# Differential heads of an encoder block: keys and values by seven products, one set of q and k

## The chip, the cores and the metric

The kernel runs on one core of a Trainium2 chip. The metric is device time in microseconds (us) of one execution, as the median of several runs. Shorthand for the engines is that of the profile: PE is TensorE (matmuls), PEld its weight loads, DVE is VectorE, ACT is ScalarE, POOL is GpSimd, SP is SyncE, which only issues DMAs here.

## The reference, cut to what matters

One residual layer on 512 tokens plus 16 meta tokens (528 rows), model width 1024, float32:

```python
xn = rmsnorm(h, norm_mix_g)
sb_q, sb_k, sb_v, df_q, df_k, df_v = split(xn @ w_in)        # six blocks of 1024 columns
# branch A: 8 stick-breaking heads of 128 columns: causal, no softmax
# branch B: 8 differential heads: two maps (c = 0, 1) of 64 columns each for q and k, one v of 128 columns
s = einsum(q, k) * 64 ** -0.5 - slope * |qpos - kpos|          # masked by chunks of 64 tokens
p = softmax(s)
w = p[:, :, 0] - lam * p[:, :, 1]
o = rmsnorm(w @ v, subln_g) * (1 - lam_init)
# both branches projected, gated, summed, w_out, residual; then SwiGLU (d_ff 2816), residual, final rmsnorm
```

## The kernel before, in words

Every float32 operand of a large product is split in two rounded parts (`split`, lines 75 to 79): ACT casts the number to `wh`, DVE subtracts to get `wl`. A product is then three matmuls (lines 272 to 274): high by high, high by low, low by high. `xT_h` and `xT_l` hold the normalised input, transposed: 8 blocks of 128 rows by 528 tokens.

The program runs through 8 stick-breaking heads, 8 differential heads (the loop `for br in range(2)` at line 984), the gates, the output projection, and the feed-forward part. While the scores, maps and outputs of head h are computed (`sb_head`, `df_head`), the projections of head h+1 are woven in as a list of units; at each `yield n` of the head generator n units are taken from the list. A differential head has:

- `scores(t)` for query blocks 0 to 2 and `scores3(c)` for block 3: matmuls of `q[c]` by `k[c]` into a PSUM tile `z`. The low parts lie in the other 64 partitions of `q[c]` and in a second row of `k[c]`, so two matmuls make a score.
- `biased`: one custom DVE instruction adds the bias and keeps the row maximum in `mx`.
- `maps(t)`: DVE negates the maximum (`nm`), ACT takes two exponentials with their sums, DVE makes the factors `rc`, scales map 0 and adds map 1.
- `attn_out`: transposes of the maps (`tr`), their split into `a_h` and `a_l`, and the product with v into another `z`.

The projections before: `halves(("df", h, 0))` makes q (24 matmuls of 512 columns), `kv_units` makes k and v, each in two halves of 264 tokens with 24 matmuls each. `q_evac` and `k_evac` write q and k from PSUM in 64-partition pieces (ACT the high part, DVE the low part), and when the last half of k is there, two DMAs on POOL's queue copy each `k[c]` into the other 64 partitions (`dk<-dk`, line 665). The scores of the head wait for those copies. Even heads keep q and k in `qh`, `ql`, `kh`, `kl` of the pool `att`; odd heads in one tile `dqk` in the place named `y_df`, so there are two sets.

From stick-breaking head 2 on (`SEVEN = 2`), k and v are made together by `seven_units`, a 2 by 2 block scheme with seven half-size products instead of eight (the blocks are the halves of the 1024 rows of the weights, the two matrices v and k, and the two halves of the tokens). Its weight operands are sums of weight blocks: `c1` splits the v chunk as it is, `c2` makes two sums on DVE and splits them, `c3` a third, `c4` a fourth (half a chunk). The token sums lie in `tA` and `tB`. A product is 12 matmuls of 264 columns. `seven_units` gives four units, u1 to u4; the DVE row `L219` is the second addition of `c2`, which reads the v chunk.

Weight chunks (512 KB) come in the order of the list `stream` by DMAs on SP's queue: `wst` has 3 places, `wsu` one place for the k chunk of a head with seven products. A place is free when the last split that reads it is done. The split parts have 4 places (`wh`, `wl`).

`y_units` are the branch projections of finished heads: ACT copies a PSUM tile to `y_out` (8 places, in the tile `y_sb`; `ys` and `sg` alternate before `y_out` exists), and POOL's queue adds it to a sum in DRAM. POOL's queue also issues `ds` transfers (line 137): sums of down-projection weights made by DMA in DRAM, one at every second unit until their list is empty, each held back until the split last written in the program has been cast.

The order on each engine is set by the framework's scheduler, which sorts by priority with its own estimate of durations. `tc.high_priority(offset=EVAC)` moves PSUM evacuations ahead. Each engine then works through its queue strictly in order, and so do the queues of SP and POOL.

## Time and profile before

| | us |
|---|---|
| median of 3 runs | 967.77 (967.52 to 967.91) |
| profiled execution, its own time | 967.45 |
| its span in the profile | 965.7 |
| PE busy | 948.0 (98%) |
| DVE busy | 705.2 (73%) |
| ACT busy | 588.9 (61%) |
| DMA engines, busy share per slice of 24 us, differential heads | 0.5 to 0.9 or more |
| from one `of` copy (line 740, once per differential head) to the next, six periods | 30.02 to 30.05 |

The page gives busy time per engine, the DMA queues, the chain of work that ended last, and the costliest groups of instructions. In a group the mean is that of one instruction; "idle before" is the time its engine stood still ahead of it. A PE row's duration includes the pipeline, so the distance of two starts, not the duration, is what a matmul costs in a row of matmuls. The differential heads run from about 261 to 500 us of the span.

### The profile page before, as it was taken

The page shows a single profiled execution, that of the slowest core. Times are in us where ns is not written, and L with a number is a line of the kernel's source. Part 1 is how long each engine was busy: PE and PEld are TensorE (multiplying, and loading weights), DVE is VectorE, ACT ScalarE, POOL GpSimd, SP SyncE. Part 2 cuts the span into 40 slices and gives each one's busy share as a digit, 9 for nine tenths or more (in the row PEclk, how much of TensorE's full clock was granted, in tenths as well). Part 3 has the DMA queues.
Part 4 walks back from the last instruction along what each step waited for, and adds up shares of the span by engine and source line. Part 5 has one row for each costly group of instructions (what it writes and reads, how often), then busy time and mean ns, then how long its engine had stood idle before and what let it go on. Part 6 is the DMA issues. An engine that isn't in the chain of part 4 may idle for free.

```text
span 965.7 us, 16166 instructions
## 1 busy us (share of the span) xinstructions
PE 948.0 (98%) x6118; PEld 853.7 (88%) x6118; DVE 705.2 (73%) x1292; ACT 588.9 (61%) x1130; POOL 185.2 (19%) x200
## 2 busy tenths in 40 slices
PE   8999999999999999999999999989999999999996
PEld 6988889898899889998888888879999999988885
DVE  7977777765577666877652553699888888999775
ACT  7765676666566666666774343585555555676564
POOL 3201111223234344322404540000000000000013
PEclk9999999999999999999999999999999999999999
DMA  8524655779989998856648853214434333276542
GB/s 243 153 71 127 184 169 177 158 164 213 189 182 188 190 205 188 187 116 123 130 112 207 272 181 104 68 46 144 115 88 123 96 108 111 67 254 204 183 156 88
DMA packets 151887, 146.88 MB, mean 152 GB/s; under 512 B 6113, under 2 KB 116866, under 8 KB 151810
## 3 DMA queue, kind: packets, MB, share of 16 engines
q1 hardware_dynamic: 132082, 98.46, 34.1%
q0 software_dynamic: 19568, 47.33, 24.3%
q8 instruction: 48, 0.79, 0.4%
q14 instruction: 29, 0.24, 0.1%
q10 hardware_dynamic: 160, 0.07, 0.0%
HBM read 122.11 MB, written 42.47 MB: 170 GB/s over the span
## 4 chain that ended last, share of the span: by engine, by line
PE 86%; DVE 8%; ACT 4%; issue 1%; DMA 0%; DVEq 0%; ACTq 0%; SPq 0%
PE mm L274 19%; PE mm L273 19%; PE mm L272 19%; PE z L272 7%; PE z L273 7%; PE z L274 7%; DVE wl L79 2%; PE z L683 1%; PE z L682 1%; PE z L538 1%; PE tr L538 1%; PE tr L514 1%; ACT wh L78 1%; DVE s L621 1%; PE z L566 1%
## 5 line engine op out<-in xcount | busy, mean ns | idle before, releaser
L272 PE MATMUL mm<-xT_h,wh 128*128 128x264 f32 (+2 forms) x656 | 214.6, 327 | 0.5 <-ACT xT_h L887 0.5
L273 PE MATMUL mm<-xT_l,wh 128*128 128x264 f32 (+2 forms) x656 | 213.3, 325 | 0.5
L274 PE MATMUL mm<-xT_h,wl 128*128 128x264 f32 (+2 forms) x656 | 212.6, 324 | 0.0
L79 DVE TENSOR_TENSOR wl<-wst,wh 128x1024 fp32r<-128x1024 f32 (+1 forms) x146 | 163.8, 1127 | 62.1 <-ACT wh L78 62.1
L78 ACT CAST wh<-wst 128x1024 fp32r<-128x1024 f32 (+1 forms) x146 | 140.0, 960 | 97.0 <-PE mm L273 64.9
L273 PEld LDWEIGHTS mm<-xT_l,wh 128*128 128x128 f32 x656 | 123.5, 188 | 10.2 <-DVE xT_l L888 1.3
L272 PEld LDWEIGHTS mm<-xT_h,wh 128*128 128x128 f32 x656 | 123.5, 188 | 9.9 <-ACT xT_h L887 0.9
L274 PEld LDWEIGHTS mm<-xT_h,wl 128*128 128x128 f32 x656 | 123.4, 188 | 9.9
L273 PE MATMUL mm<-hT_l,wh 128*128 128x256 f32 x284 | 80.5, 284 | 0.7 <-DVE hT_l L1133 0.7
L272 PE MATMUL mm<-hT_h,wh 128*128 128x256 f32 x284 | 80.3, 284 | 0.6 <-DVE sg L1228 0.6
L274 PE MATMUL mm<-hT_h,wl 128*128 128x256 f32 x284 | 80.1, 283 | 0.0
L1350 POOL TENSOR_TENSOR outs<-hres,gF 128x512 f32<-128x512 f32 x4 | 7.3, 1815 | 283.1 <-DVE hres L1336 278.0
L137 POOL DMA_DIRECT2D ds<-in_w_ffn_down_dram x36 | 28.5, 792 | 153.8 <-ACT wh L78 124.0
L686 DVE CUSTOM_DVE_ANT_0 pr<-z,bias 128x144 f32<-128x144 f32 (+3 forms) x64 | 30.9, 502 | 35.0 <-PE z L683 34.9
L273 PEld LDWEIGHTS mm<-hT_l,wh 128*128 128x128 f32 x284 | 53.7, 189 | 1.1 <-DVE hT_l L1133 1.1
L272 PEld LDWEIGHTS mm<-hT_h,wh 128*128 128x128 f32 x284 | 53.4, 189 | 0.9 <-DVE sg L1228 0.8
L274 PEld LDWEIGHTS mm<-hT_h,wl 128*128 128x128 f32 x284 | 53.5, 189 | 0.0
L272 PE MATMUL mm<-o_h,wh 128*128 128x512 f32 x128 | 53.1, 415 | 0.0
L272 PE MATMUL z<-wh,da 128*128 128x512 f32 (+1 forms) x132 | 50.9, 386 | 0.3 <-DVE hres L1336 0.3
L274 PE MATMUL mm<-o_h,wl 128*128 128x512 f32 x128 | 50.8, 397 | 0.0
L273 PE MATMUL mm<-o_l,wh 128*128 128x512 f32 x128 | 50.1, 392 | 0.3 <-DVE o_l L754 0.3
L273 PE MATMUL z<-wl,da 128*128 128x512 f32 (+1 forms) x132 | 50.2, 381 | 0.0
(346 smaller groups left out, 2562.7 us busy)
## 6 DMA issues: line engine op xcount, KB each, us to landing
wst<-in_w_in_dram SPq DMA_DIRECT2D x40, 512.0 KB, 5.9
ds<-in_w_ffn_down_dram POOLq DMA_DIRECT2D x30, 512.0 KB, 4.8
wst<-in_w_ffn_gate_dram SPq DMA_DIRECT2D x22, 512.0 KB, 4.0
wsu<-in_w_ffn_up_dram SPq DMA_DIRECT2D x21, 512.0 KB, 3.9
wst<-in_w_gate_dram SPq DMA_DIRECT2D x16, 512.0 KB, 4.5
y_df<-y_out POOLq DMA_DIRECT2D x32, 256.0 KB, 6.0
slots<-ds SPq DMA_DIRECT2D x13, 512.0 KB, 3.4
ds<-ds POOLq DMA_DIRECT2D x10, 512.0 KB, 7.4
```

The lines of the kernel that those rows point to most:

```text
L78: cast["last"] = (hi_copy or nc.scalar.copy)(hi, src)
L79: (lo_eng or nc.vector).tensor_tensor(lo, src, hi.bitcast(F32), op=ALU.subtract)
L137: tc.add_manual_dep(nc.gpsimd.dma_start(dst, src, **kw).ins, cast["last"].ins.name, paced)
L272: nc.tensor.matmul(ps, lhsT=ah, rhs=bh, start=(start and i == 0), stop=False, skip_group_check=skip)
L273: nc.tensor.matmul(ps, lhsT=ah, rhs=bl, start=False, stop=False, skip_group_check=skip)
L274: nc.tensor.matmul(ps, lhsT=al, rhs=bh, start=False, stop=(stop and i == n - 1), skip_group_check=skip)
L514: nc.tensor.transpose(pt[:, j * P:(j + 1) * P], vT[:, j * P:(j + 1) * P], ident)
L538: nc.tensor.transpose(pt[:, (t - j) * P:(t - j + 1) * P], blocks(t, j * P, (j + 1) * P), ident)
L566: nc.tensor.matmul(ps.rearrange("p (t q) -> p t q", q=P)[:, :, lo_rows:P], lhsT=vf[:, 1], rhs=a_s[:, 0:4 * qn], start=False, stop=True)
L621: nc.vector.tensor_tensor_scan(f, f, f, 0.0, op0=ALU.add, op1=ALU.bypass)
L682: nc.tensor.matmul(o, lhsT=q[c][:, qs], rhs=k[c][:, 0, k0:k1], start=True, stop=False)
L686: nc.vector.tensor_tensor_reduce(po, zz, bb, scale=1.0, scalar=-3.0e38, op0=ALU.add, op1=ALU.max, accum_out=mx[:, t, c:c + 1])
```

## The change

k and v of all eight differential heads are made by `seven_units`: chunks are streamed in the order v, k, q, with `c4` prepared right behind `c3`. q is projected after k and v instead of before. There is one set of q and k, in the pool `att`, for even and odd heads alike. `y_df` holds the token sums until the last head; `y_out` is made there only in the last iteration, so y tiles of the earlier ones go through `ys` and `sg`. Since `k_evac` in this scheme writes the second token half first, the copy DMAs are issued with the first half (`s.start == 0`). `seven_units` gives -k for that scheme's factor, hence the negated scores: `biased` scales by -1 and keeps a minimum, the exponentials use `scale=-1.0` and the minimum as bias, and the negation `nm` on DVE is gone. Map 0 is scaled on ACT instead of DVE.

```diff
-        for i in range(3):
+        for i in (2, 1, 0):
             cols(("df", h, i), w_in, (3 + i) * D + h * P)
...
     def sevens(key):
-        return key[0] == "sb" and key[1] >= SEVEN
+        return key[0] == "df" or key[0] == "sb" and key[1] >= SEVEN
...
-            fns = [c1, c2, c3] if key[2] else [generic, c4]
+            with_k = key[0] == "df"
+            fns = [c1, c2, c3] + [c4] * with_k if key[2] else [generic] + [c4] * (not with_k)
...
-        if h % 2:
-
-            both = opool.tile([P, 4 * L + 2 * SEQ], F32R, tag="y_df", name="dqk", bufs=1)
...
+        q = [ap_.tile([P, SEQ], F32R, tag=("qh", "ql")[c], name=f"dq{c}") for c in range(2)]
+        k = [ap_.tile([P, 2, L], F32R, tag=("kh", "kl")[c], name=f"dk{c}") for c in range(2)]
...
-                if s.stop == L:
+                if s.start == 0:
                     nc.gpsimd.dma_start(k[c][hs[1 - c]].bitcast(F32), k[c][a].bitcast(F32))
...
-        return d, halves(("df", h, 0), xT, QT, q_evac) + kv, turn
+        return d, kv + halves(("df", h, 0), xT, QT, q_evac), turn
...
-            nc.vector.tensor_tensor_reduce(po, zz, bb, scale=1.0, scalar=-3.0e38, op0=ALU.add, op1=ALU.max,
+            nc.vector.tensor_tensor_reduce(po, zz, bb, scale=-1.0, scalar=3.0e38, op0=ALU.add, op1=ALU.min,
...
-            nm = small.tile([P, 2], F32, tag="nm", name="nm")
-            nc.vector.tensor_scalar(nm, mx[:, t], -1.0, None, op0=ALU.mult)
             for c in range(2):
-                nc.scalar.activation(pr[:, c], pr[:, c], AF.Exp, bias=nm[:, c:c + 1], accum_out=ls[:, t, c:c + 1])
+                nc.scalar.activation(pr[:, c], pr[:, c], AF.Exp, scale=-1.0, bias=mx[:, t, c:c + 1], accum_out=ls[:, t, c:c + 1])
...
-                nc.vector.tensor_scalar(pr[:, 0], pr[:, 0], rc[:, 0:1], None, op0=ALU.mult)
+                nc.scalar.activation(pr[:, 0], pr[:, 0], AF.Copy, scale=rc[:, 0:1])
...
-            y_out.append(xtp.tile([P, KT, SEQ], F32, tag="y_sb", name="y_out"))
...
             if turn is None:
+                y_out.append(opool.tile([P, KT, SEQ], F32, tag="y_df", name="y_out", bufs=1))
```

The scheduler's order changes with it, in three places that the prediction speaks of. Line numbers of the changed kernel are lower by 5 to 8 from `df_units` on (scores L677 and L678 are L682 and L683 before), and matmuls L273 to L275 are L272 to L274 before.

**PE, first scores of the next head.** `mm_3814` and `mm_3823` are y units, `z_3844` the first score tile of the next head. Before:

```order
L565 MATMUL z_3794<-a_f_3634,vf_3416 128x128
L566 MATMUL z_3794<-a_s_166,vf_3416 128x4x64
L272 MATMUL mm_3814<-o_h_2496,wh_3669 128x512
L273 MATMUL mm_3814<-o_l_2497,wh_3669 128x512
L274 MATMUL mm_3814<-o_h_2496,wl_3670 128x512
...
L682 MATMUL z_3844<-dk0_3471,dq0_3469 128x256
L683 MATMUL z_3844<-dk0_3471,dq0_3469 128x256
L682 MATMUL z_3844<-dk1_3472,dq1_3470 128x256
```

Here the scores stand behind the product with v (`z_3794`) and the last y units. Now, at the same place of the program (`z_3859` is the score tile, `mm_3752` and `mm_3762` y units, `z_3804` the product with v):

```order
L274 MATMUL mm_3752<-o_l_2497,wh_3686 128x512
L275 MATMUL mm_3752<-o_h_2496,wl_3687 128x512
L273 MATMUL z_3804<-a_h_3663,vh_3425 128x512
L677 MATMUL z_3859<-dk0_3481,dq0_3479 128x256
L273 MATMUL mm_3762<-o_h_2496,wh_3686 128x512
L274 MATMUL mm_3762<-o_l_2497,wh_3686 128x512
L275 MATMUL mm_3762<-o_h_2496,wl_3687 128x512
L273 MATMUL mm_3762<-o_h_2496,wh_3686 128x512
```

One score matmul has moved ahead of 40 others: six of a y unit, twelve transposes, the ten that are left of the product with v, and twelve of two y units. It is held until the copy of `dk0` has landed and `dq0` is written, and PE takes its queue in order. This is so for heads 1 to 7.

**DVE, behind the last score of a head.** Before, k's low parts (L662) and one split (L79) stand here, and q's (L655) stand well ahead:

```order
L662 SCALAR_TENSOR_TENSOR dk0_3471<-mm_3635,dk0_3471 64x264
L713 RECIPROCAL rc_3627<-ls_3477 128x2
L714 TENSOR_TENSOR rc_3627<-rc_3627,cn_171 128x2
L662 SCALAR_TENSOR_TENSOR dk1_3472<-mm_3635,dk1_3472 64x264
L715 TENSOR_SCALAR pr_3481<-pr_3481,rc_3627 128x528
L716 SCALAR_TENSOR_TENSOR pr_3481<-pr_3481,rc_3627 128x528
L79 TENSOR_TENSOR wl_3947<-wst_3667,wh_3946 128x1024
L541 TENSOR_TENSOR a_l_3633<-tr_3725,a_h_3632 128x512
```

Now (`wl_3749`, `wl_3898`, `wl_3903` are the splits of `c1`, `c2`, `c3` for the head after the next):

```order
L79 TENSOR_TENSOR wl_3749<-wst_3525,wh_3748 128x1024
L657 SCALAR_TENSOR_TENSOR dk0_3481<-qq_3524,dk0_3481 64x264
L657 SCALAR_TENSOR_TENSOR dk1_3482<-qq_3524,dk1_3482 64x264
L706 RECIPROCAL rc_3658<-ls_3487 128x2
L657 SCALAR_TENSOR_TENSOR dk0_3481<-mm_3520,dk0_3481 64x264
...
L233 TENSOR_TENSOR wst_3525<-s21_3894,wst_3525 128x512
L79 TENSOR_TENSOR wl_3903<-wsu_3625,wh_3902 128x1024
L650 SCALAR_TENSOR_TENSOR dq0_3479<-mm_3703,dq0_3479 64x512
L542 TENSOR_TENSOR a_l_3664<-tr_3733,a_h_3663 128x512
```

A split now stands ahead of each of the writes that the next scores need: `wl_3749` ahead of `dk0`, `wl_3903` ahead of `dq0`.

**DVE, in the middle of a head.** Before, the last factor of the normalised output (L752) is followed by the next maximum:

```order
L751 SCALAR_TENSOR_TENSOR sq_3444<-tr_3534,var_max_173,sq_3444 128x512
L686 ISA pr_3480,mx_3476<-z_3543,bias_3474 128x400
L686 ISA mx_3476 128x1
L752 TENSOR_TENSOR of_3443<-of_3443,sq_3444 128x512
L708 TENSOR_SCALAR nm_3550<-mx_3476 128x2
```

Now the second addition of `c2` stands there, which reads the v chunk `wst_3525` of the head after the next:

```order
L744 SCALAR_TENSOR_TENSOR sq_3452<-tr_3566,var_max_173,sq_3452 128x512
L681 ISA pr_3490,mx_3486<-z_3575,bias_3484 128x400
L681 ISA mx_3486 128x1
L745 TENSOR_TENSOR of_3451<-of_3451,sq_3452 128x512
L219 TENSOR_TENSOR s21_3894<-s21_3894,wst_3525 128x512
L706 RECIPROCAL rc_3584<-ls_3487 128x2
L681 ISA pr_3491,mx_3486<-z_3619,bias_3484 128x528
```

The row L219 has come in, with a factor and a maximum of the current head behind it.

More of the change, by code (lines that the diff above doesn't have):

```diff
@@ L640, in df_units @@
         hs = (slice(0, 64), slice(64, 128))
-        if h % 2:
-            both = opool.tile([P, 4 * L + 2 * SEQ], F32R, tag="y_df", name="dqk", bufs=1)
-            q = [both[:, 4 * L + c * SEQ:4 * L + (c + 1) * SEQ] for c in range(2)]
-            k = [both[:, 2 * c * L:2 * (c + 1) * L].rearrange("p (a l) -> p a l", a=2) for c in range(2)]
-        else:
-            q = [ap_.tile([P, SEQ], F32R, tag=("qh", "ql")[c], name=f"dq{c}") for c in range(2)]
-            k = [ap_.tile([P, 2, L], F32R, tag=("kh", "kl")[c], name=f"dk{c}") for c in range(2)]
+        q = [ap_.tile([P, SEQ], F32R, tag=("qh", "ql")[c], name=f"dq{c}") for c in range(2)]
+        k = [ap_.tile([P, 2, L], F32R, tag=("kh", "kl")[c], name=f"dk{c}") for c in range(2)]
         d["q"], d["k"] = q, k
```

## The prediction

> **What bounds the kernel now.** I read the page first, its busy times and its chain:
>
> ```profile
> span 965.7 us, 16166 instructions
> PE 948.0 (98%) x6118; PEld 853.7 (88%) x6118; DVE 705.2 (73%) x1292; ACT 588.9 (61%) x1130; POOL 185.2 (19%) x200
> PE 86%; DVE 8%; ACT 4%; issue 1%; DMA 0%; DVEq 0%; ACTq 0%; SPq 0%
> ```
>
> PE is busy nearly all the span and holds 86% of the chain. Next I cut the differential heads at their `of` copies and asked for busy time by stretch (columns: stretch, its length, then busy us of PE, PEld, DVE, ACT and POOL with counts, granted clock, DMA share, GB/s):
>
> ```profile
> 321.22:351.24 30.02, 30.02 (x199) 27.49 (x198) 21.09 (x55) 19.83 (x48) 11.96 (x13) 1.00 0.96 180
> 351.24:381.29 30.05, 30.05 (x199) 27.51 (x198) 21.09 (x55) 19.83 (x47) 11.23 (x13) 1.00 0.86 187
> 411.31:441.37 30.06, 30.06 (x199) 27.50 (x198) 21.09 (x55) 19.83 (x48) 8.75 (x9) 1.00 0.55 122
> ```
>
> A head takes 30.03 us and PE never rests in it, so its matmuls set its length. DVE and ACT have 9 and 10 us to spare. The DMA engines have almost none while the `ds` sums are made (0.96, 0.86), and some after them (0.55). The profiled execution took 967.45 us, 1.75 around its span, and 0.3 below the median of the runs; the sum is made against 967.45. About 0.2% (1.9 us) is what a measurement here tells from no change.
>
> **Matmuls removed.** k and v of a head are 4 halves of 24 matmuls, 96 in all; seven products of 12 are 84. All have 264 columns. Their price is the distance of starts in the timeline of PE:
>
> ```profile
> 422.00 0.28 PE L272 MATMUL mm<-xT_h,wh 128*128 128x264 f32 x1
> ...
> 424.91 0.28 PE L682 MATMUL z<-dqk 128*128 128x264 f32 x1
> ...
> 434.07 0.93 PE L538 MATMUL tr<-ident,pr 128*128 128x128 f32 x7
> 434.76 0.48 PE L272 MATMUL mm<-o_h,wh 128*128 128x512 f32 x1
> ...
> 437.60 0.38 PE L538 MATMUL tr<-ident,pr 128*128 128x128 f32 x2
> ...
> 444.87 0.40 PE L272 MATMUL mm<-xT_h,wh 128*128 128x512 f32 x1
> ...
> 447.62 0.39 PE L747 MATMUL tr<-sql,ones_r 128*128 128x512 f32 x1
> ```
>
> 24 matmuls lie between the first two rows: (424.91 - 422.00) / 24 = 0.121 us each. A y matmul costs (437.60 - 434.76) / 12 = 0.237, one of q (447.62 - 444.87) / 12 = 0.229, seven transposes 0.69. Removed: 8 heads x 12 x 0.121 = 11.6 us of PE. If nothing else waits, a head takes 30.03 - 1.45 = 28.58.
>
> **Work added on DVE and ACT.** By group (mean ns before the bar between idle times):
>
> ```profile
> L79 DVE TENSOR_TENSOR wl<-wst,wh 128x1024 fp32r<-128x1024 f32 x4 | 4.9, 1223 | 2.0 <-ACT wh L78 2.0
> L78 ACT CAST wh<-wst 128x1024 fp32r<-128x1024 f32 x4 | 4.2, 1051 | 4.8 <-PE mm L273 4.8
> L662 DVE SCALAR_TENSOR_TENSOR dk<-mm,dk 64x264 fp32r<-64x264 f32 x4 | 1.7, 430 | 0.1
> L655 DVE SCALAR_TENSOR_TENSOR dq<-mm,dq 64x512 fp32r<-64x512 f32 x2 | 1.4, 688 | 0.1
> L710 ACT ACTIVATE pr<-pr,nm 128x528 f32<-128x528 f32 x2 | 1.4, 723 | 0.0
> L708 DVE TENSOR_SCALAR nm<-mx 128x2 f32<-128x2 f32 x4 | 0.7, 165 | 0.0
> L715 DVE TENSOR_SCALAR pr<-pr,rc 128x528 f32<-128x528 f32 x1 | 0.5, 495 | 0.0
> L219 DVE TENSOR_TENSOR s<-s,wst 128x512 f32<-128x512 f32 x27 | 18.6, 690 | 0.6
> L429 DVE TENSOR_TENSOR vT<-mm,qq 128x264 f32<-128x264 f32 x6 | 2.6, 433 | 19.4 <-ACT e L616 19.4
> ```
>
> Splits: k and v took two per head, the sums take three and a half. Per head DVE gains 1.5 x 1.22 (splits), 4 x 0.69 (weight sums) and 3 x 0.43 (evacuations), 5.9 in all. It loses four `nm` (0.66) and four scalings of at most 0.495 (up to 2.0): 3.2 to 5.2 more, at most 26.3 of 28.58. ACT gains 1.5 x 1.05, about 0.4 for one more copy, and four scalings; no row shows these on ACT, they lie between nothing and four of the widest exponential (2.9), and I take 2.3: 24.1 of 28.58. Neither engine fills up, so these sums cost nothing in themselves while PE is ahead of both; what they stand in front of in a queue does. Negated scores change no duration, and the y tiles in `ys` and `sg` have a head's length to be sent.
>
> **First wait: the hoisted score.** In heads 1 to 7 a score matmul of the next head now stands between two y units and needs `dq0` and the landed copy of `dk0`. For `dq0`: the cast of `c3` needs the parts' place that q's weights hold, so it starts after q's last matmul; then come ACT's cast 1.05, DVE's split 1.22, DVE's `dq0` 0.69, some 0.3 of hops between engines (an estimate): 3.3 us. PE in that time has seven transposes, six y matmuls and one more: 0.69 + 1.42 + 0.23 = 2.3. So PE waits 0.9 us per head whatever the DMAs do.
>
> For `dk0`: `c1`'s cast needs the place that the last product of k holds. From the last k matmul: cast 1.05, split 1.22, three pieces of k 1.29, and some 0.45 (an estimate) for a small row and the hops, so the copy is issued after 4.0 us. PE gets to the score after 0.23 + 12 x 0.121 + 20 x 0.229 + 2.3 = 8.6 us. The copy has 4.6 us to land. What it takes is in the DMA view, first for the stretch with `ds` (290 to 410 us), then for the one without (410 to 470; last column, median us from issue to landing), then all copies of odd heads, and POOL's queue around one:
>
> ```profile
> wst<-in_w_in_dram SPq DMA_DIRECT2D x12, 512.0 KB, 10.4
> ds<-ds POOLq DMA_DIRECT2D x10, 512.0 KB, 7.4
> dk<-dk POOLq DMA_DIRECT2D x4, 264.0 KB, 8.2
> dqk<-dqk POOLq DMA_DIRECT2D x4, 264.0 KB, 8.7
> ...
> dk<-dk POOLq DMA_DIRECT2D x2, 264.0 KB, 5.0
> dqk<-dqk POOLq DMA_DIRECT2D x2, 264.0 KB, 5.7
> ...
> DMA to landing us min/median/max: 2.9/6.6/10.0
> ...
> 369.89 0.95 POOL L137 DMA_DIRECT2D ds<-ds  x1
> 371.36 0.57 POOL L665 DMA_DIRECT2D dk<-dk  x1 [0.52 <-DVE dk L662]
> ```
>
> The copies are issued 1.5 us behind a `ds` transfer and land after it. Before, nothing showed of it: scores came a third of a head later. Now, for the five heads with a `ds` in front (the queue keeps that order), 8.6 would mean a wait of 4.0. I take less, a landing of 6.9 and a wait of 2.3, halfway between 5.0 and 8.7: longer heads thin the traffic, and the weight load that was issued beside the copy falls elsewhere. Ends: 0.9 and 4.1. The two heads without `ds`: 0.9 (the floor; 5.7 would give 1.1). Together 5 x 2.3 + 2 x 0.9 = 13.3, ends 6.3 and 22.7.
>
> The Trainium skill, "DMA: Bandwidth & Descriptors", section "Anatomy of one DMA — SWDGE (gpsimd) path", fits one transfer from GpSimd as 2.0 us plus its bytes over 436e3 per us, an estimate of 2.6 us for 264 KB. By it the copy lands in time, and the seven heads pay the floor alone (rival A). The trace disagrees, with 5.0 to 8.7.
>
> **Second wait: the v chunk.** A v chunk's place in `wst` is free after `c4`'s split, about where a load starts now, 357.07. DVE adds with it right behind the output factor, which begins at 361.13 now:
>
> ```profile
> 357.07 0.37 SPq L189 DMA_DIRECT2D wst<-in_w_in_dram  x1
> ...
> 361.13 0.69 DVE L752 TENSOR_TENSOR of<-of,sq 128x512 f32<-128x512 f32 x1
> ...
> DMA to landing us min/median/max: 7.3/7.3/7.3
> DMA to landing us min/median/max: 11.5/11.5/11.5
> DMA to landing us min/median/max: 10.9/10.9/10.9
> DMA to landing us min/median/max: 6.4/6.4/6.4
> DMA to landing us min/median/max: 6.8/6.8/6.8
> DMA to landing us min/median/max: 5.9/5.9/5.9
> ```
>
> The last six rows are the loads issued at this place of heads 0 to 5. The allowance is 361.82 - 357.07 = 4.7 us, and about 0.9 more since ACT now scales two maps ahead of it: 5.6. Before, a load had most of a head. Behind the addition stand the factor of the third map and a maximum, for which ACT waits, and behind ACT's next row the copy that PE needs before the product a22. Counted from the end of the first two score blocks (444.87, or 354.8 three heads earlier), the addition begins at 361.82 + 0.9 - 354.8 = 7.9; behind it come 0.69, about 1.0 for maximum and factor, and 0.9 on ACT: 10.5. PE gets to a22 after 60 product matmuls (7.3), three of q (0.7) and the norm and score matmuls (about 2): 10.0. So PE has nothing to spare there, and a late load delays it by the same amount. With landings as before: 1.7 + 5.9 + 5.3 + 0.8 + 1.2 + 0.3 = 15.2. I take 11, with the two longest at about 3.5 each, since a head that waits spreads its bytes over more time; ends 0 and 15.2.
>
> **Sum.** -11.6 + 13.3 + 11 = +12.7: 967.45 + 12.7 = 980. Ends: -11.6 + 6.3 + 0 = -5.3 (962), and -11.6 + 22.7 + 15.2 = +26.3 (994).
>
> **Rivals.** A, faster: copies and v chunks land in time. For it speaks that the quickest copies of the trace took 2.9 us, and that the DMA share falls when heads stretch; against it the medians above. All seven heads pay the floor of 0.9: 962. It decides if copies land within 4.6 + 0.9 = 5.5 us of issue. If even the floor hides, 956.
>
> B, no change: the waits come to about the 11.6 saved, as with landings of 6 us and one late chunk: 7 x 1.4 + 2 = 11.8, 967.5.
>
> C, much slower: landings as long as before, 994, or PE's clock falls after a long wait. No stretch here shows a granted clock below 1.00, because PE never rests. If the clock halved for as long as the wait, five waits of 4.0 would cost 5 x 2.0 more on top of about 980: 990. The Trainium skill, "TensorE: Matmul & The Clock Gate", Part 1, has the clock halve after an idle window of about 3.4 us; no run here shows whether 2 to 4 us within a busy stretch do it.
>
> That the matmuls do not go is excluded: PE's queue is 96 rows shorter.
>
> **How the numbers follow.** The forecast (both waits, 969.5 to 988) has 0.74, A 0.12, B 0.05, C 0.09. Range 963 to 992: below lies the better part of A, above it most of C, together some 0.15. Likeliest case alone: 971 to 988. Faster by over 0.2%: 0.12; within: 0.05; slower: 0.83.
>
> **What would show it.** Right: heads of 31 to 34 us in the stretch with `ds` and about 30 after it; PE idle time ahead of the score line (L677), released by the copies or DVE's `dq`, near 13 us in all; DVE idle ahead of L219, released by DMA, in heads 0 to 2; PE idle ahead of a product for ACT's `qq` copy. DVE 24 to 26 and ACT 23 to 25 us of summed work per head. Wrong: PE idle-free heads of 28.6, copies landing under 5.5 us, or waits on ACT and DVE with no DMA behind them.

## The result, and the profile after

The changed kernel takes 998.87 us, the median of 4 runs (995.72 to 1004.5). The kernel before took 967.84 on the same chip. The ratio is 1.0313, 95% interval 1.0281 to 1.0346: 31 us slower, where the prediction said 12.7. The profiled execution is the fastest of the four, 995.72 us. Its page, the busy times and the chain:

```profile
span 993.9 us, 16096 instructions
PE 953.6 (96%) x6022; PEld 848.2 (85%) x6022; DVE 730.2 (73%) x1300; ACT 619.4 (62%) x1186; POOL 186.1 (19%) x200
PE 71%; DVE 12%; DMA 8%; ACT 6%; issue 2%; ACTq 0%; DVEq 0%; SPq 0%
```

The 96 matmuls are gone (6118 to 6022), and yet PE is busy for 5.6 us more. Its share of the chain fell from 86% to 71%; DMA, at 0% before, has 8%. The same cut at the heads' output copies as in the prediction, now from the last stick-breaking head on (the second row is differential head 0, the last one shown is head 7; columns as there, the granted clock third from the end):

```profile
230.90:267.50 36.60, 30.19 (x185) 26.32 (x184) 22.50 (x34) 20.18 (x38) 8.86 (x10) 0.95 0.76 147
267.50:304.70 37.20, 31.89 (x191) 28.38 (x190) 23.57 (x55) 22.26 (x53) 10.53 (x12) 0.91 0.83 170
304.70:336.40 31.70, 29.39 (x187) 25.97 (x187) 24.44 (x56) 23.72 (x55) 13.03 (x13) 1.00 0.93 180
...
367.90:398.30 30.40, 29.23 (x187) 25.91 (x186) 24.34 (x56) 23.48 (x55) 11.62 (x13) 1.00 0.80 187
...
460.60:494.00 33.40, 30.81 (x187) 27.03 (x186) 22.09 (x52) 23.69 (x54) 10.68 (x13) 0.95 0.89 210
494.00:521.00 27.00, 27.00 (x137) 22.65 (x136) 15.68 (x40) 21.57 (x46) 7.44 (x8) 1.00 0.60 120
```

Two stretches stand out, the last stick-breaking head and differential head 0. The same two in the kernel before:

```profile
230.30:261.10 30.80, 29.45 (x198) 26.46 (x197) 17.34 (x25) 18.43 (x36) 7.82 (x9) 1.00 0.95 196
261.10:291.20 30.10, 30.10 (x203) 27.63 (x201) 20.28 (x54) 18.32 (x47) 10.60 (x12) 1.00 0.91 192
```

The first took 30.8 us and takes 36.6, the second took 30.1 and takes 37.2. Heads 1 to 5 take 30.4 to 31.7, head 6 takes 33.4. Of the rows shown after the change, the granted clock is below 1.00 in just the three long ones. What PE waited for between 200 and 530 us (before: two waits, 1.6 us):

```profile
PE z L677 <- DMA dk<-dk: 5.0, 4, 2.0
PE z L677 <- DVE o_l L636: 4.3, 1, 4.3
PE mm L273 <- DVE qq L442: 3.8, 1, 3.8
PE mm L273 <- ACT qq L441: 3.4, 3, 1.4
PE z L677 <- DVE a_l L542: 2.8, 2, 1.6
PE mm L273 <- DVE vT L430: 2.6, 1, 2.6
PE z L273 <- ACT a_h L541: 1.0, 1, 1.0
PE z L677 <- DVE dq L650: 0.6, 1, 0.6
```

The three waits for VectorE's `o_l`, `qq` and `vT`, 10.7 us in all, are in the two long stretches. VectorE's own timeline says why (idle time and what ended it in brackets):

```profile
245.27 0.69 DVE L219 TENSOR_TENSOR s<-s,wst 128x512 f32<-128x512 f32 x1 [9.90 <-DMA wst<-in_w_in_dram]
245.87 0.69 DVE L226 TENSOR_TENSOR wsu<-wst,wsu 128x512 f32<-128x512 f32 x1
246.48 0.43 DVE L430 TENSOR_TENSOR vT<-mm,qq 128x264 f32<-128x264 f32 x1
...
274.18 0.69 DVE L218 TENSOR_TENSOR s<-wsu 128x512 f32<-128x512 f32 x1 [7.29 <-DMA wsu<-in_w_in_dram]
274.90 0.69 DVE L636 TENSOR_TENSOR o_l<-z,o_h 128x512 fp32r<-128x512 f32 x1
```

The weight sum L219 at 245 belongs to differential head 1, whose products PE needs some 30 us later. It stands early in VectorE's queue all the same, and VectorE waits 9.9 us for its v chunk with `vT` and the scans of the running head behind it. In the next head L218, again a sum for a later head, waits 7.3 us for its k chunk in front of `o_l`, the low part of the last stick-breaking head's output. PE's side of the second case, and the two loads in the chain (start, duration):

```profile
271.02 0.28 PE L678 MATMUL z<-dk,dq 128*128 128x256 f32 x1
275.65 0.60 PE L677 MATMUL z<-dk,dq 128*128 128x272 f32 x1 [4.35 <-DVE o_l L636]
```

```profile
235.39 9.78 DMA wst<-in_w_in_dram
...
264.12 9.97 DMA wsu<-in_w_in_dram
```

Each load was issued late. The v chunk's place is freed by the split of `c4`, the last VectorE instruction ahead of L219, so VectorE saw the whole transfer. The k chunk's place is freed by the split of `c3`; VectorE came to L218 2.8 us after that load's issue and saw 7.3 of its 10 us.

Then the clock. Its records change at whole multiples of 3.413 us, and the stretches below are cut there (PE's busy time is the first pair after the length):

```profile
242.80:246.21 3.41, 1.67 (x12) 1.24 (x11) 0.94 (x2) 1.09 (x2) 2.11 (x2) 1.00 0.64 123
246.21:249.63 3.42, 1.93 (x13) 1.70 (x13) 3.42 (x7) 0.00 (x0) 0.00 (x0) 1.00 1.02 175
485.16:488.57 3.41, 1.66 (x7) 1.21 (x8) 2.81 (x5) 1.56 (x4) 0.93 (x1) 1.00 1.13 240
488.57:491.98 3.41, 3.41 (x16) 2.65 (x15) 0.88 (x3) 1.61 (x6) 0.88 (x1) 0.50 0.79 184
669.48:672.89 3.41, 1.67 (x12) 1.46 (x13) 3.41 (x4) 3.38 (x4) 0.00 (x0) 1.00 0.07 19
672.89:676.30 3.41, 3.41 (x16) 3.30 (x16) 2.24 (x4) 1.05 (x2) 0.61 (x1) 0.50 0.71 213
```

In the second and third pair PE is busy for 1.66 and 1.67 us of a window, and the next has half clock. A wait of 1.6 us and the end of another are enough (485.16). The window from 669.48 holds most of two waits of 1.1 and 1.0 us that the kernel before has too; there the same two fell into two windows, which PE filled to 2.28 and 2.47 us, and cost nothing more. The first pair shows the edge: 1.67 busy and no fall. I counted PE's idle time in every such window at full clock between 40 and 930 us, in the profiled executions of all kernels of this study: 4354 windows. The 39 with half clock behind them had 1.74 us idle or more, the other 4315 had 1.75 or less; the two ranges overlap by 0.02 us, and the ends of matmuls are modelled. In the changed kernel four stretches make 17.1 us at half clock.

A third loss is behind the heads, where nothing was edited: 472.9 us from the last output copy to the end, 467.4 before. One line of the last product's matmuls, of the changed kernel and then of the kernel before (the durations are min/median/max in ns):

```profile
L273 PE MATMUL z<-wh,da x132: 279/393/505, 873.9 to 984.4; 128*128 128x512 f32 x121, 128*128 128x256 f32 x11
```

```profile
L272 PE MATMUL z<-wh,da x132: 281/389/497, 848.5 to 957.1; 128*128 128x512 f32 x121, 128*128 128x256 f32 x11
```

The distance of starts says it better: the 512-column matmuls on `o_h`, `o_l`, `mg` and `da` start every 232.6 ns on average (961 of them), 227.9 before (959). In the two programs, as they were built, these tiles differ in their SBUF address alone: the dropped tile `nm` of negated maxima took 128 bytes per partition, and these tiles, allocated behind it, begin 128 bytes lower now.

### The profile page after: what moved, and what is told of

It reads as the page before. It is cut to its first block, busy times and chain, and to the rows that moved or that the text cites. A ratio compares the mean times of both kernels' runs of the same rounds, so it can differ in the third digit from the quotient of the medians.

```text
span 993.9 us, 16096 instructions
## 1 busy us (share of the span) xinstructions
PE 953.6 (96%) x6022; PEld 848.2 (85%) x6022; DVE 730.2 (73%) x1300; ACT 619.4 (62%) x1186; POOL 186.1 (19%) x200
## 3 DMA queue, kind: packets, MB, share of 16 engines
q1 hardware_dynamic: 132082, 98.46, 33.2%
## 4 chain that ended last, share of the span: by engine, by line
PE 71%; DVE 12%; DMA 8%; ACT 6%; issue 2%; ACTq 0%; DVEq 0%; SPq 0%
PE mm L274 15%; PE mm L273 15%; PE mm L275 15%; PE z L273 6%; PE z L274 6%; PE z L275 6%; DMA wst<-in_w_in_dram 4%; DVE wl L79 3%; DMA dk<-dk 2%; ACT wh L78 2%; DMA wsu<-in_w_in_dram 1%; ACT pr L703 1%; DMA wst<-in_w_gate_dram 1%; PE z L539 1%; PE tr L515 1%
## 5 line engine op out<-in xcount | busy, mean ns | idle before, releaser
L79 DVE TENSOR_TENSOR wl<-wst,wh 128x1024 fp32r<-128x1024 f32 (+1 forms) x146 | 161.0, 1107 | 48.8 <-ACT wh L78 47.6
L78 ACT CAST wh<-wst 128x1024 fp32r<-128x1024 f32 (+1 forms) x146 | 136.5, 936 | 71.3 <-PE mm L274 37.8
L273 PE MATMUL mm<-xT_h,wh 128*128 128x512 f32 (+2 forms) x496 | 170.3, 345 | 4.3 <-DVE qq L442 3.8
L274 PE MATMUL mm<-xT_l,wh 128*128 128x512 f32 (+2 forms) x496 | 169.1, 341 | 0.5
L275 PE MATMUL mm<-xT_h,wl 128*128 128x512 f32 (+2 forms) x496 | 168.4, 340 | 0.0
L273 PEld LDWEIGHTS mm<-xT_h,wh 128*128 128x128 f32 x496 | 94.7, 191 | 14.0 <-DVE qq L442 4.0
L274 PEld LDWEIGHTS mm<-xT_l,wh 128*128 128x128 f32 x496 | 94.8, 191 | 10.1 <-DVE xT_l L881 1.3
L275 PEld LDWEIGHTS mm<-xT_h,wl 128*128 128x128 f32 x496 | 94.7, 191 | 9.6
L274 PE MATMUL mm<-hT_l,wh 128*128 128x256 f32 x284 | 81.0, 286 | 0.7 <-DVE hT_l L1126 0.7
L273 PE MATMUL mm<-hT_h,wh 128*128 128x256 f32 x284 | 80.8, 286 | 0.5 <-DVE sg L1221 0.5
L275 PE MATMUL mm<-hT_h,wl 128*128 128x256 f32 x284 | 80.6, 285 | 0.0
L273 PE MATMUL mm<-o_h,wh 128*128 128x512 f32 x128 | 53.6, 418 | 2.6 <-DVE vT L430 2.6
L274 PEld LDWEIGHTS mm<-hT_l,wh 128*128 128x128 f32 x284 | 54.3, 191 | 1.2 <-DVE hT_l L1126 1.1
L218 DVE TENSOR_TENSOR s<-wsu 128x512 f32<-128x512 f32 x35 | 25.0, 714 | 40.9 <-DMA wsu<-in_w_in_dram 30.4
L273 PEld LDWEIGHTS mm<-hT_h,wh 128*128 128x128 f32 x284 | 54.0, 191 | 1.0 <-DVE sg L1221 0.7
L275 PEld LDWEIGHTS mm<-hT_h,wl 128*128 128x128 f32 x284 | 54.2, 191 | 0.0
L78 ACT CAST wh<-wsu 128x1024 fp32r<-128x1024 f32 x35 | 36.8, 1050 | 24.6 <-PE mm L274 23.2
L273 PE MATMUL z<-wh,da 128*128 128x512 f32 (+1 forms) x132 | 51.2, 388 | 0.3 <-DVE hres L1329 0.3
L275 PE MATMUL mm<-o_h,wl 128*128 128x512 f32 x128 | 51.3, 401 | 0.0
L274 PE MATMUL mm<-o_l,wh 128*128 128x512 f32 x128 | 50.9, 398 | 0.3 <-DVE o_l L747 0.3
```

The lines of the kernel that those rows point to most:

```text
L78: cast["last"] = (hi_copy or nc.scalar.copy)(hi, src)
L79: (lo_eng or nc.vector).tensor_tensor(lo, src, hi.bitcast(F32), op=ALU.subtract)
L218: nc.vector.tensor_tensor(s[:, K2], u[:, K1], u[:, K2], op=ALU.add)
L273: nc.tensor.matmul(ps, lhsT=ah, rhs=bh, start=(start and i == 0), stop=False, skip_group_check=skip)
L274: nc.tensor.matmul(ps, lhsT=ah, rhs=bl, start=False, stop=False, skip_group_check=skip)
L275: nc.tensor.matmul(ps, lhsT=al, rhs=bh, start=False, stop=(stop and i == n - 1), skip_group_check=skip)
```

## The experiments

Times are medians; each ratio is to the kernel before in runs on the same chip. Lines of an experiment's profile stand up to 11 further down than those of the changed kernel. The expectations call the stick-breaking heads softplus heads. Padded means with the 128 bytes of the first experiment.

**Addresses: put back, and moved in the kernel before.**

```diff
     small = ctx.enter_context(tc.tile_pool(name="small", bufs=4))
+    small.tile([P, 32], F32, name="pad_s", bufs=1)
```

> The changed kernel with an unused tile of 128 bytes per partition in the pool of small tiles, where the dropped tile for the negated maxima stood: every later SBUF address is again what it was before. Theory 'addresses': in the changed kernel the 512-column matmuls of the output factor's products, the merge and the last stage start every 232 ns, in the kernel before every 227 ns; they go back to 227, which gives about 3.4 us behind the last head and some 0.1 us in each head, 994 to 995. Theory 'waits and clock alone': the addresses mean nothing, about 999 as without it.

> The kernel before, with the same unused 128 bytes added: nothing else changes, only later SBUF addresses move by 128 bytes the other way. Theory 'addresses' (a step of 128 bytes matters, in either direction): the same matmuls go from 227 to 232 ns, 3.5 to 5 us slower, 971.5 to 973. Rival: it stays at 967.8.

The padded changed kernel takes 994.8 us (1.0283, 1.0265 to 1.03), 4.1 less. The kernel before with the same line takes 971.77 (1.0045, 1.0028 to 1.0061), 3.9 more. The row of the first and of the second:

```profile
L274 PE MATMUL z<-wh,da x132: 281/389/497, 871.8 to 981.6; 128*128 128x512 f32 x121, 128*128 128x256 f32 x11
```

```profile
L273 PE MATMUL z<-wh,da x132: 274/392/500, 850.9 to 961.4; 128*128 128x512 f32 x121, 128*128 128x256 f32 x11
```

Starts are 227.9 and 232.3 ns apart. Shown in both directions: 128 bytes of address cost this kernel 4 us.

**Transfers: no `ds` while the sums are tight.**

```diff
-                    tick(*RATE[br])
+                    if (br, h) < (0, 7):
+                        tick(*RATE[br])
...
-            tick(1, 1)
+            for _ in range(3):
+                tick(1, 1)
```

> The changed kernel with no weight-sum transfers (ds) issued from the last softplus head on until the feed-forward part, which then issues up to three at each of its steps. Theory 'late loads': the chunk loads of 512 KB that took about 10 us here land in 5 to 6, VectorE's waits of 9.9 us (L219, last softplus head) and 7.3 us (L218, first head of the changed kind) shrink to under 3, PE's waits of 6.4 and 5.3 us in these two stretches and the halved clock behind them mostly go, and the copies of dk0 land in 5: 978 to 985. Theory 'the hoisted score alone': only the waits for the copies shrink, 5.0 to about 1: 994 to 996. If places and not bandwidth hold the loads up: no change, 997 to 1000.

1003.82 us (1.0361, 1.0324 to 1.0397): a miss in the total. In the heads the theory of late loads holds in part: the last output copy starts at 505.3 us instead of 521.0, and heads 1 to 6 take 29.8 to 30.8. The wait at L219 shrank to 6.8, not to under 3; that at L218 in head 0 shrank to 1.3. The transfers, put off, then collided with the feed-forward part:

```profile
664.00:760.00 96.00, 82.86 (x645) 81.64 (x644) 63.92 (x101) 41.35 (x69) 19.71 (x21) 0.93 0.99 207
```

The DMA share is 0.99 and PE rests for 13 us there. Contention makes the loads long, but they are waited for without it too.

**Only heads 1 to 7 by sevens.**

```diff
-        return key[0] == "df" or key[0] == "sb" and key[1] >= SEVEN
+        return key[0] == "df" and key[1] > 0 or key[0] == "sb" and key[1] >= SEVEN
...
-        for i in (2, 1, 0):
+        for i in (2, 1, 0) if h else (1, 2, 0):
             cols(("df", h, i), w_in, (3 + i) * D + h * P)
...
-                if s.start == 0:
+                if s.start == 0 if h else s.stop == L:
```

> The changed kernel, but differential head 0 makes its keys and values by the generic products (12 matmuls of 0.121 us more, 1.45 us); heads 1 to 7 by seven. Theory 'the first head of the kind pays, because its chunks come from the softplus heads' places': the two stretches of 36.7 and 37.2 us go back to about 31 and 31: 987 to 989. Theory 'the adds wait for any load of this kind': the waits move on to head 1, whose first adds stand in the same place, and the gain is half or less: 993 to 999.

988.72 us (1.0214, 1.0192 to 1.0236), 10.2 less. The total fits the first theory, the trace only half of it: the last stick-breaking head is back at 29.4 us, but head 0 still takes 36.4, with 7.5 us of VectorE at L218 and 4.36 of PE for `o_l`, and heads 1 and 4 now take 34.6 and 35.2. The wait is not tied to the first head of the kind.

**The first sum behind `vl`** (padded). The added dependence only orders two instructions of one engine.

```diff
-        nc.vector.tensor_tensor(s[:, K2], u[:, K1], u[:, K2], op=ALU.add)
+        add = nc.vector.tensor_tensor(s[:, K2], u[:, K1], u[:, K2], op=ALU.add)
+        if isinstance(f, tuple) and f[0] == "df":
...
+            tc.add_manual_dep(add.ins, cast["vl"].ins.name, behind)
...
+            cast["vl"] = nc.vector.tensor_tensor(vl, pv[:, 0:3], vh.bitcast(F32), op=ALU.subtract)
```

> The changed kernel with the 128 bytes (994.8), and one order more: VectorE's first weight sum of a differential head (c2, L218) stands behind the low part of the values of the head in front (vl), which is two thirds of a head later than the scheduler had put it. Theory 'place in the queue': the sums stood up to 35 us ahead of the products that need them, directly behind the issue of their loads, and blocked everything behind them on VectorE for 7 to 10 us; now the loads have landed when VectorE comes to them, PE's waits of 6.2 and 5.6 us in the last softplus head and the first differential head go, with the halved clock behind them, and part of the smaller ones: 978 to 984. Theory 'late loads': the place of the k chunk is freed later too, so the next load starts later and the wait moves with it: 990 to 996.

992.99 us (1.0254, 1.0227 to 1.0281): hardly a gain in the total (1.8 us). The last stick-breaking head takes 29.0 us, and of VectorE's waits for a load at the sums one of 2.8 us is left. ScalarE took the waiting over, in four heads (6.5, 9.0, 5.0 and 3.5 us); the longest in ScalarE's timeline:

```profile
309.92 0.39 ACT L660 ACTIVATE dk<-mm 64x264 fp32r<-64x264 f32 x1
319.28 1.04 ACT L79 CAST wh<-wst 128x1024 fp32r<-128x1024 f32 x1 [8.98 <-DMA wst<-in_w_in_dram]
```

This is the cast of `c1`, again for a later head and again ahead of its load, with the last map's exponential behind it.

**A second place for the k chunk** (padded).

```diff
-            st = fpools["a"].tile([P, KT, P], F32, tag="wsu", name="wsu")
+            st = fpools["a"].tile([P, KT, P], F32, tag="wsu", bufs=2, name="wsu")
...
-        return opool.tile([P, XP], F32, tag=f"sg{br}", name="sg")[:, 0:SEQ]
+        return opool.tile([P, L], F32, tag=f"sg{br}", name="sg")[:, 0:SEQ]
...
-                    ys = ap_.tile([P, SEQ], F32, tag="ys", bufs=2, name="ys")
+                    ys = ap_.tile([P, SEQ], F32, tag="ys", bufs=1, name="ys")
```

> The changed kernel with the 128 bytes (994.8), and a second place for the k chunk (wsu, two buffers); the room comes from one place less for y tiles (ys) and from gate tiles without their unused columns. Theory 'the load starts too late for want of a place': VectorE's waits at L218 (21.9 us in all, 7.3 the longest) go, the first differential head comes down from 37.4 to about 32; the 9.9 us at L219 in the last softplus head stay, since the v chunk has no second place: 985 to 989. Theory 'place in the queue': the sum is put earlier in the queue by as much as the load is, and waits for it there: 992 to 997. One place of y tiles less may cost ACT a wait of 1 to 2 us per head.

987.84 us (1.0206, 1.0182 to 1.023), as the first theory said: head 0 comes down to 31.9 us, the last stick-breaking head stays at 37.8, since the v chunk got no more room:

```profile
DVE s L220 <- DMA wst<-in_w_in_dram: 15.3, 6, 9.9
```

**The score no longer hoisted** (padded; `cast["y"]` is the last y matmul).

```diff
+            if t == c == 0 and "y" in cast:
...
+                tc.add_manual_dep(first.ins, cast["y"].ins.name, behind)
```

> The changed kernel with the 128 bytes (994.8), and each head's first score matmul held behind the last y matmul of the head in front, so that PE meets dk0 and dq0 one y unit (2.8 us) later. By the prediction's first wait (13.3 us at the score line) these waits go: 982 to 985. By the trace after, where PE waits 5 us for the copies and 0.6 for dq at that line, and with the clock that falls behind a wait of 2 us: 987 to 990. If the time is lost on VectorE alone: 993 to 996.

1002.25 us (1.0349, 1.0312 to 1.0386): 7.5 more, against every theory, my prediction's first. The waits for the copies are gone, but PE now waits for VectorE's maxima at the scores of block 3, which need a PSUM place back:

```profile
PE z L679 <- DVE mx L686: 11.3, 5, 3.5
```

VectorE is late with them, since it stands for loads at the weight sums (L218 and L219 of the changed kernel) that its queue holds ahead of the maxima:

```profile
DVE s L219 <- DMA wsu<-in_w_in_dram: 37.5, 8, 7.4
DVE s L220 <- DMA wst<-in_w_in_dram: 19.1, 6, 10.1
```

In the padded kernel these two waits are 20.3 and 12.9 us. So this run does not show what the hoist is worth by itself; why the sums wait longer for their loads here stays open.

**Negated scores and ScalarE's scaling alone**, in the kernel before with `nm`'s 128 bytes kept.

> The kernel before with two parts of the change alone: negated scores (no negated maxima on VectorE), and the first map scaled on ScalarE; the 128 bytes of the dropped tile are kept as an unused tile. No sevens, two sets of q and k. Theory 'these parts cost nothing' (VectorE and ScalarE have room in the differential heads): 967 to 969. Rival: the scaling, which ScalarE now does behind VectorE's reciprocal, sets back the third map and the turns of a head, 0.3 to 1 us a head: 970 to 976.

967.3 us (0.9988, 0.9976 to 0.9999). These parts cost nothing.

**Both instructions behind their loads** (padded, with the late sum).

```diff
         split(wh, wl, g)
+        if isinstance(f, tuple) and f[0] == "df" and "a_h" in cast:
...
+            tc.add_manual_dep(cast["last"].ins, cast["a_h"].ins.name, behind)
```

> The changed kernel with the 128 bytes (994.8), c2's first sum behind vl as in the run with the late sum (992.99), and now also ScalarE's cast of the v chunk (c1) behind the first turns (a_h) of the head in front. In that run ScalarE stood for 9.0 us ahead of this cast, for a load issued 17 us earlier, with the exponentials of the last map behind it, and PE waited 4.4 to 9.1 us for that map in four heads. Theory 'place in the queue': with both instructions behind their loads nothing stands in front of a load any more; heads of 29 to 30 us throughout, 963 to 969. Theory 'the transfers are too many for the time': the next instruction that needs a chunk takes the wait over, 980 to 992.

973.6 us (1.006, 1.0044 to 1.0077): two orders on two engines take 21.2 us away. Heads 0, 1, 2 and 6 in its profile:

```profile
259.20:288.50 29.30, 29.30 (x190) 26.22 (x189) 24.05 (x57) 21.83 (x54) 10.51 (x12) 1.00 0.94 181
288.50:322.40 33.90, 30.93 (x187) 27.21 (x186) 25.47 (x58) 23.45 (x54) 13.74 (x13) 0.95 0.94 178
322.40:351.60 29.20, 29.19 (x187) 25.91 (x187) 23.42 (x56) 23.33 (x54) 11.75 (x13) 1.00 0.95 185
439.40:474.90 35.50, 31.25 (x189) 26.99 (x188) 26.34 (x57) 25.24 (x57) 11.85 (x13) 0.95 0.79 195
```

With the DMA engines at 0.94, heads 0 and 2 run without a wait: a full DMA share is no loss where nothing stands in a queue ahead of its load. The other two wait behind two more casts, `c1`'s (3.1 us) and that of the first gate chunk (3.8).

**The `ds` transfers in the stick-breaking heads, without and with the two orders** (padded).

```diff
-RATE = (1, 2), (1, 2)
+RATE = (3, 4), (0, 1)
```

> The changed kernel with the 128 bytes (994.8); the weight-sum transfers (ds) are issued at three of four units of the softplus heads instead of one of two, and at none in the differential part. In the run without them up to the feed-forward part, the last output factor's product ended 15.7 us earlier than in the changed kernel (505.3 against 521.0) and the feed-forward part lost 17. Theory 'contention': the differential part gains those 15 us again and the softplus heads, whose 28.0 us show no PE wait, swallow 6 transfers a head instead of 4: 977 to 982. Rival: the softplus heads get the waits instead, 985 to 995.

> Both edits together: the two instructions behind their loads, and the weight-sum transfers in the softplus heads alone. If queue places and contention are the whole loss beside the addresses: the 96 matmuls (11.6 us) come through except for some 0.5 us a head (dq0's wait, small waits for qq): 959 to 964. If the hoisted score still costs a wait for the copies of dk0 as predicted: 965 to 970.

982.97 us (1.0155, 1.0138 to 1.0172), and with the orders 968.4 (1.0007, 0.9982 to 1.0032; 963.83 to 977.26). The first misses its range by 1 us, still short of its rival's; the second lies in the range of its second theory, but not for that theory's reason, since its profile lists no wait of PE for the copies of `dk`. In both profiles a stick-breaking head now waits: head 5, 30.2 us alone and 34.8 with the orders, instead of 28.0. Three transfers in four units seem too dense.

**The two casts moved, without and with a pause of the transfers** (padded, with the late sum).

```diff
+        if isinstance(f, tuple) and f[0] == "df" and "dq" in cast:
...
+            tc.add_manual_dep(cast["last"].ins, cast["dq"].ins.name, behind)
...
+        if n > at_of["df", NH - 1, 0] and stream[n][0][0] == "gate":
...
+            tc.add_manual_dep(cast["last"].ins, cast["dq"].ins.name, behind)
```

The second run adds this:

```diff
-                    tick(*RATE[br])
+                    if not (0, 6) < (br, h) < (1, 2):
+                        tick(*RATE[br])
```

> The run with the sum and the cast behind their loads (973.6), with the two casts that still waited moved: c1's cast stands behind dq1 (ScalarE, about 2 us later; its load landed 3.1 us after the cast's turn in differential head 1), and the cast of the gate chunk, which waited 3.8 us in head 6, also behind dq1. Theory 'place in the queue': these two stretches come down from 33.9 and 35.5 us to about 29.5 and 30, with the halved clock behind them: 963 to 966, less than before. Rival 'transfers': the wait goes to what comes next (the generic casts, dk's copies): 969 to 973.

> The same, and no weight-sum transfers issued from the last softplus head to differential head 1; they follow at one of two units in heads 2 to 7. If queue places settle it all: the same as without this edit, 963 to 966. If the transfers still hold something up in head 1 (four ds, four loads and six other transfers in 30 us): 2 to 4 us less than without it. The ones that follow in heads 5 to 7 could make the gate chunk late again: up to 3 us more.

966.56 us (0.998, 0.9963 to 0.9997) and 973.66 (1.005, 1.003 to 1.007). The casts' places gave 7 us in the median, and the kernel is about level with the one before (0.8 us less). The first misses its range by 0.6 us: in its profile, an execution of 969.93 us, the two stretches come to 32.6 and 33.2 us, not to 29.5 and 30. Pausing the transfers took head 1 from 32.6 us to 29.1, and head 6 from 33.2 to 40.2: the transfers that were put off meet the gate chunk there, as the expectation feared, at more than twice its price.

**The gate cast at the end of head 6, without and with transfers spread anew.** The gate cast now stands behind `of`, and where the branch projection's weights for head 5 are taken, preparation runs one step ahead instead of two:

```diff
-        prepare(prep_at[key] + (READY if at < at_of["df", 0, 0] else 2))
+        prepare(prep_at[key] + (READY if at < at_of["df", 0, 0] else 1 if key == ("y_df", 5) else 2))
```

The second run also has the pause, and `RATE = (5, 8), (1, 2)`.

> The run of 966.56 with the cast of the gate chunk set behind the copy of head 6's output (of), that is at the end of its head. Theory 'place in the queue': head 6 comes from 33.2 to about 30, its halved clock goes, head 1 stays at 32 to 34: 962 to 965. Rival: the first gate product of the last head now waits for its weights, and head 7 gives it back: 966 to 969.

> The same, with the weight-sum transfers at five of eight units up to softplus head 6, none from softplus head 7 to differential head 1, one of two after. Theory 'queue places and, in head 1, transfers are all': heads of 29.1 to 30 throughout, 959 to 962, clearly under the kernel before (967.3). Rival: five of eight are too dense for the softplus heads (at three of four, head 5 waited 4.5 to 6.3 us), 963 to 968.

967.18 us (0.9993, 0.9979 to 1.0008) and 964.0 (0.9967, 0.9953 to 0.998). The first misses its range and lies in its rival's, but head 7, in which the rival had the gain lost, takes 26.2 us (27.9 in the run of 966.56): in its profile head 6 falls to 29.7, while in heads 1 and 2 PE waits 1.2 and 2.4 us. The second is the one version that is faster than the kernel before by more than 0.2%: by 3.2 us. Its median is 2 us above its theory's range and inside its rival's, but the rival's reason is not in its profile, where stick-breaking heads 2 to 6 take 27.9 us, as before (27.9 to 28.1). Stretches of heads 0, 1, 3, 6 and 7:

```profile
259.10:288.30 29.20, 29.20 (x190) 26.16 (x189) 24.32 (x57) 21.88 (x54) 7.43 (x9) 1.00 0.65 136
288.30:317.40 29.10, 29.10 (x187) 25.87 (x186) 24.88 (x57) 23.42 (x54) 9.41 (x9) 1.00 0.57 123
...
346.50:376.20 29.70, 29.36 (x187) 25.95 (x187) 24.77 (x57) 23.42 (x54) 11.81 (x13) 1.00 0.83 192
...
435.00:465.10 30.10, 29.41 (x187) 25.94 (x187) 23.75 (x55) 23.56 (x55) 13.54 (x15) 1.00 0.98 220
465.10:491.30 26.20, 26.20 (x135) 22.15 (x133) 14.30 (x39) 20.76 (x46) 7.73 (x8) 1.00 0.71 148
```

No head falls below full clock in this execution, which took 961.9 us; its runs lie between 961.07 and 968.2.

## Why the prediction was right or wrong

Wrong in its size: slower, as forecast, but beyond the range. Between the two profiled executions lie 995.72 - 967.45 = 28.3 us, which the traces split so: matmuls -11.6; listed waits of PE +21.9 (23.5 less 1.6); half clock +7.5 (17.1 us, less 2.1 in which PE stood anyway, halved); addresses +4.5 (961 x 4.7 ns). That is 22.3. The other 6 are an estimate by difference: delays too short to be listed. The last experiment's heads show such delays too (29.1 to 30.1 us against the 28.58 of the matmuls): in its head 1, where PE never rests, the starts of 264-column, y and q matmuls lie 0.14, 0.25 and 0.13 us further apart in all than in the kernel before.

- **Matmuls removed, -11.6:** the rows are gone. No head came to 28.58; the best took 29.1.
- **Work on VectorE and ScalarE:** at most 26.3 and 24.1 us a head forecast, 22.1 to 25.1 and 22.3 to 23.7 measured in heads 0 to 6. Neither fills. Negated scores and ScalarE's scaling cost nothing (967.3).
- **First wait, 13.3:** the mechanism was there, the size was not. PE waited 5.0 us for the copies in four heads (the longest 2.0) and 0.6 for `dq`. The mis-sized term is the landing of 6.9 taken for all five heads with `ds`. The copies of heads 2 to 7 landed in 4.4, the median, and the four that PE waited for in 4.8 to 6.4 (the second fence is from the chain, start and duration):

```profile
dk<-dk POOLq DMA_DIRECT2D x12, 264.0 KB, 4.4
```

```profile
293.02 6.44 DMA dk<-dk
326.00 5.12 DMA dk<-dk
357.83 4.77 DMA dk<-dk
418.20 6.19 DMA dk<-dk
```

  The floor of 0.9 for `dq` measured 0.4 to 0.6 in the run without `ds`. Where no sum or cast stands ahead of its load, the hoisted score costs next to nothing: PE's listed waits in the last experiment have none at the score line. The Trainium skill, "DMA: Bandwidth & Descriptors", section "Anatomy of one DMA — SWDGE (gpsimd) path", has a fit that gives an estimate of 2.6 us for such a copy; the trace's 4.4 lies between it and my 6.9.
- **Second wait, 11:** this is the step that failed and that put the time outside the range, as the prediction put it: "A v chunk's place in `wst` is free after `c4`'s split [...] DVE adds with it right behind the output factor". I worked out one sum, L219, in heads 0 to 5, as if VectorE's queue were the same everywhere. L218 and its k chunk got nothing, and neither did the last stick-breaking head. The path that I costed is in the trace, but small: VectorE waits 0.2, 1.3 and 1.5 us at L219 in heads 0 to 2, and PE 3.4 us for ACT's `qq` in three heads. What I left out is larger. The sums are ordered a head or so ahead of their use, and two of them met a 10 us load with the running head's work behind them: L219 one head earlier than I looked, and L218 in head 0. PE waited 10.7 us there, and with the half clock behind these waits the two stretches alone are 5.8 and 7.1 us longer. The late-sum run shows the place in the queue as the cause of the first (29.0 us); the run with room for the k chunk shows that an earlier load cures the second (31.9).
- **Rival C:** it had 0.09, for landings as long as before or a falling clock. The clock fell, but not by long waits alone, as I had it: by waits that fill half of a fixed window. The sum had nothing for it; it cost 7.5 us. The four runs of the changed kernel lie 9 us apart, in the order of their mean clock (0.990, 0.987, 0.984 and 0.979).
- **Not in any step:** the 128 bytes. The diff drops `nm`, and I costed its instructions, not its place: 4.1 us, shown both ways.
- **What would show it:** heads of 31 to 34 us with `ds`: 30.4 to 31.7, but 37.2 for head 0; about 30 after it: 30.9 and 33.4. PE at the score line by copies and `dq` near 13 us: 5.6. VectorE ahead of L219 in heads 0 to 2: 2.9 in all, but 9.9 in the head before them.

What stays open: what the operands' addresses do to each other inside PE, what holds up the matmuls by the last 0.5 to 1.5 us of a head, and what the hoist is worth by itself.

## What to carry to other kernels

Before costing work that is added to an engine with idle time, find where each added instruction will stand in that engine's queue, whose load it needs, and what stands behind it: an instruction ordered a head too early turns a hidden transfer into a wait of the whole core, and ordering two instructions behind their loads gave 21 of the 31 us back. Cost the waits twice, once as themselves and once by the half clock that followed here whenever a 3.4 us window was half empty. And when an edit drops a tile, look at which addresses move.

## What was not expected of the hardware

- The clock: in all 39 windows of 3.413 us with half clock behind them PE was idle for 1.74 us or more; in the other 4315, with full clock behind them, for 1.75 or less. The Trainium skill, "TensorE: Matmul & The Clock Gate", Part 1, has a free-running window of 3413 ns, with which the records agree. It also has the clock halve after at least one idle window; here half an idle window was enough.
- Addresses: moving one operand's tiles by 128 bytes, with the weights `wh` and `wl` where they were, changed the distance of 512-column matmuls from 227.9 to 232.6 ns. In the faster programs, as built, both operands' tiles begin 64 bytes past a multiple of 256, in the slower ones one of them 192 past. The 512-column matmuls on `xT`, whose address never moved, stayed at 228 in all. Other offsets were not tried.
- Two loads of 512 KB took 9.8 and 10.0 us of the chain while `ds` transfers ran. Without those transfers VectorE's wait for the first was 6.8 us instead of 9.9.
